# Spectra in DRAM regrouped by residue, natural blocks stored two at a time, and the filters' weights first in their pool

## The chip, the cores and the metric

The kernel runs on one core of a Trainium2 chip. The metric is device time in microseconds, from one launch, as the median of several runs; lower is better. A core has TensorE (PE in the profile; PEld are its weight loads), VectorE (DVE), ScalarE (ACT), GpSimd (POOL) and SyncE (SP). SP computes nothing: it issues DMA transfers. ScalarE issues some as well, in order with its own work. All transfers share 16 DMA engines.

## The reference

One layer of an encoder over 2048 positions and 1024 channels, float32: a projection feeds a long-convolution branch (Hyena, 512 channels) and an mLSTM branch; then come an output projection, cross-attention and a feed-forward block. The change touches the long convolution and one kind of output of the projection.

```python
def _hyena_filter_spectrum(L, w1, b1, fr1, w2, b2, fr2, w3):
    ...
    hid = jnp.sin(fr1 * (z @ w1 + b1))          # z: features of the position, (L, 33)
    hid = jnp.sin(fr2 * (hid @ w2 + b2))        # (L, 64)
    filt = (hid @ w3).reshape(L, HYENA_ORDER, FILTER_DIRS, D_HYENA)
    filt = filt * jnp.exp(-t * jnp.abs(deltas))[:, None, None, :]
    ...
    return jnp.fft.rfft(two_sided, axis=0)

def _hyena(hy, spec, skip):
    z, g1, g2 = u[..., :D_HYENA], u[..., D_HYENA:2 * D_HYENA], u[..., 2 * D_HYENA:]
    for o, gate in enumerate((g1, g2)):
        conv = jnp.fft.irfft(jnp.fft.rfft(z, n=2 * L, axis=1) * spec[:, o], n=2 * L, axis=1)[:, :L]
        z = gate * (conv + z * skip[o])
    return z
```

## The kernel before, in words

The transform of length 4096 is done by TensorE in two steps, with position n = 64 a + 16 q + j (a from 0 to 31, q from 0 to 3, j from 0 to 15). The first step (`front` for the filters, `spectrum` for the signal) transforms over a: for each j and q it gives 64 rows k (the frequency's low part, real and imaginary), 512 channels wide. The second step works by blocks, one for each k pair, with a 128 x 128 matrix over the 64 values of (q, j), real and imaginary. Between the steps the data must be regrouped from "by j" to "by k". That is done through DRAM: the tensors `fs0`, `fs1` hold the filters' spectra, `zs0`, `zs1` the signal's and `zg0`, `zg1` the product on its way back, 4 MB each, in the shape (64 k, 16 j, 4 q, 512).

- `by_phase` moves a piece between a tile of [128, 2, 512] (two values of j, 64 rows k each, two values of q) and DRAM. It issues two transfers of 64 partitions, 256 KB each, one for each j. It stores `fs` (in `front`, SP's queue) and `zs` (in `spectrum`, half on ScalarE's queue), and loads `zg` (in `load3`, SP).
- `of_block` names the block of one frequency: 64 rows (j, q) of 2 KB. A tile of [128, 2, 512] holds two blocks m = 0, 1, with the real part in partitions 0 to 63 and the imaginary part in 64 to 127. `load_filter` (`fs`) and `load2` (`zs`) fill such a tile with two transfers over 64 partitions, each with a half of both blocks; `back` stores `zg` with two, once both blocks are done.
- `natural` makes outputs of the projection in their natural layout, 128 positions by 256 columns at a time. Each is copied from PSUM to a tile `st` (three buffers, shared with `sweep_out`) and stored by ScalarE's queue with a transfer of 128 KB.
- `filters` makes the filters, and its tiles lie in the pool `f_sb`. `fw` are its weights and `hid` its hidden layer; both are last read by the products at L325. The tiles `a` (seven buffers) are the last to be stored. When `filters` ends the pool is closed, and the pool `h_sb` of `hyena` is opened at the same addresses: first `f1`, `e2` and `ghy`, then its ten buffers `a`, the first of which take the input tiles z. Tiles lie in a pool in the order in which they are first asked for.

The work of several generators is woven together by hand (`weave`, with weights), and a scheduler with a model of time then orders each engine's instructions and inserts semaphores. The main stream at that time is `sweep` and `natural`, the projection's products (L357, L360, L361), with the loads of `w_in` (`wn`, L397) and of the input (`xt`, L526) on SP's queue; `memproj` follows it (L726, its copies at L711). Each engine and each queue runs its own list in order.

Of the kernel before, what the change touches and what calls it, by code (L numbers as in the profile page):

```python
# [10 lines left out]
F32 = mybir.dt.float32  # L11
# [10 lines left out]
CH = 512  # L22
# [6 lines left out]
def shape_constants():  # L29
    f32 = np.float32  # L30
    ang = f32(TWO_PI / L) * np.arange(L, dtype=f32)
    tl = np.linspace(0.0, 1.0, L, dtype=f32)
    bands = np.linspace(1e-4, 15, 16, dtype=f32)
    arg = bands[:, None] * ang[None, :]
    feat = np.concatenate([tl[None], np.cos(arg), -np.sin(arg)], axis=0).astype(f32)
    back = (L - np.arange(L)) % L
    c_feat = np.concatenate([feat, feat[:, back]], axis=0)

    lo = math.log(1e-2) / 1.5
    hi = math.log(1e-2) / 0.3  # L40
    deltas = np.abs(np.linspace(lo, hi, CH, dtype=f32))
    win = np.exp(-(tl[:, None] * deltas[None, :]).astype(np.float64)).astype(f32)
    winb = win[back].copy()
    winb[0] = 0.0
    c_win = np.stack([win, winb], 0).reshape(2, 32, 4, 16, CH).transpose(0, 2, 1, 3, 4).reshape(2, L, CH)

    n1 = np.arange(32)
    kk = np.arange(16)
    f1 = np.zeros((2, 32, 4, 16, 2, 4))
    for par in range(2):  # L50
        th = 2 * np.pi * ((n1[:, None] * (2 * kk + par)[None, :]) % 64) / 64
        for h in range(4):
            f1[par, :, h, :, 0, h] = np.cos(th)
            f1[par, :, h, :, 1, h] = -np.sin(th)
            if par == 0:
                f1[0, :, h, 0, 1, h] = 1.0 - 2.0 * (n1 % 2)
    f1 = f1.reshape(2, 128, 128)
    wgt = np.full((2, 16, 2, 4), 2.0)
    wgt[0, 0] = 1.0
    e2 = f1.transpose(0, 2, 1) * (wgt.reshape(2, 128, 1) / 4096.0)  # L60
    own = f1.reshape(2, 32, 4, 16, 2, 4)[:, :, 0, :, :, 0].transpose(1, 0, 2, 3).reshape(32, 64)
    inv = e2.reshape(2, 16, 2, 4, 32, 4)[:, :, :, 0, :, 0].reshape(64, 32)

    n2 = np.arange(64).reshape(4, 16).T.reshape(64)
    k2 = np.arange(64)

    def block(freq):
        th = 2 * np.pi * ((n2[:, None] * freq[None, :]) % 4096) / 4096
        return np.cos(th), np.sin(th)

    dm = np.zeros((32, 2, 64, 2, 64))
    for par in range(2):
        for k in range(16):
            k1 = 2 * k + par
            b = dm[par * 16 + k]
            if k1 > 0:
                c, s = block(k1 + 64 * k2)
                b[0, :, 0], b[1, :, 0], b[0, :, 1], b[1, :, 1] = c, s, -s, c
            else:
                c, s = block(64 * k2[:32])  # L80
                b[0, :, 0, :32], b[0, :, 1, :32] = c, -s
                b[0, :, 1, 0] = 1.0 - 2.0 * (n2 % 2)
                c, s = block(32 + 64 * k2[:32])
                b[1, :, 0, 32:], b[1, :, 1, 32:] = c, -s
    dm = dm.reshape(32, 128, 128)
    em = dm.transpose(0, 2, 1).copy()
    two = np.full((128, 1), 2.0)
    two[0] = two[64] = 1.0
    em[0] *= two
    c = {  # L90
        "c_feat": c_feat,
        "c_win": c_win,
        "c_f1": np.tile(own, (4, 1)),
        "c_e2": np.tile(inv, (2, 1)),
        "c_dm": dm.transpose(1, 0, 2),
        "c_em": em.transpose(1, 0, 2),
    }
    return {k: np.ascontiguousarray(v.astype(np.float32)) for k, v in c.items()}
# [30 lines left out]
class Prog:  # L129
# [101 lines left out]

    def filters(self):
        nc, tc, a = self.nc, self.tc, self.a
        sd = [self.dram(f"fs{o}", (64, 16, 4, CH)) for o in range(2)]
        sb, ta, tb = self.fsb, self.ta, self.tb
        if True:
            fw = sb.tile([128, 1280], F32, name="fw")
            nc.sync.dma_start(out=fw, in_=a["fw"])
            w1, w2, w3 = fw[0:66, 0:128], fw[:, 128:256], fw[:, 256:1280].rearrange("p (o c) -> p o c", o=2)
            par = self.par[:, 128:132]  # L240
            for i in (0, 2):
                nc.vector.tensor_tensor(self.fb[:, i:i + 1], par[:, i:i + 1], par[:, i + 1:i + 2], ALU.mult)
            f1 = sb.tile([128, 128], F32, name="f1")[:, 0:64]
            nc.sync.dma_start(out=f1, in_=a["c_f1"])

            def sine(dst, src, b, fr, first=False):
# [10 lines left out]
                nc.vector.tensor_scalar(u, u, -PI_F, PI_F, ALU.max, ALU.min)  # L257
                nc.scalar.activation(dst, u if len(dst.shape) == 2 else u.rearrange("p (n q j) -> p n q j", q=4, j=16), AF.Sin)

            hid = sb.tile([128, 16, 128], F32, name="hid")  # L260
            def feat(c):
                t = tb()
                nc.sync.dma_start(out=t[0:66], in_=a["c_feat"][:, 512 * c:512 * c + 512])
# [53 lines left out]
            for j2 in range(8):  # L317
                yield 9
                (wf, wb), nxt = nxt, windows(j2 + 1)
                for o in range(2):  # L320
                    st, es = [ta() for h in range(2)], []
# [15 lines left out]
        self.fes.close()  # L337

    def by_phase(self, queue, d, j2, h, t, load=False):
        for jj in range(2):  # L340
            at, own = d[:, 2 * j2 + jj, 2 * h:2 * h + 2], t[64 * jj:64 * jj + 64]
            queue.dma_start(out=own if load else at, in_=at if load else own)

    def filters_open(self):
        self.fes = ExitStack()
        self.fsb = self.fes.enter_context(self.tc.tile_pool(name="f_sb", bufs=1))
        self.fsb.tile([128, 32], F32, name="f_even")

    def ta(self):
        return self.fsb.tile([128, 2, CH], F32, tag="a", name="a", bufs=7)  # L350
# [510 lines left out]
    def natural(self, hf, tiles, after=None, at=4):  # L861
        nc, a, sb = self.nc, self.a, self.isb
        xh, xl = self.xh, self.xl
        win = a["w_in"][0]
        for c2 in tiles:
            n = 256 if c2 < 3 else 272
            c0 = 2560 + 256 * c2
            wh, wl = next(self.wst)
            for t in range(8):
                if t % 4 == 0:  # L870
                    yield 11
                if c2 == tiles[-1] and after is not None:
                    if after is True and t == 0:
                        nxt = self.x_chunks(0)
                    if t == at:
                        if after is True:
                            self.prepq = nxt
                        else:
                            after()
                ts = slice(128 * t, 128 * t + 128)  # L880
                r0 = 1024 * hf + 128 * t
                p = self.mm()
                for k in range(8):
                    self.mm3(p[:, :n], xh[:, k, ts], xl[:, k, ts], wh[:, k, :n], wl[:, k, :n], k == 0, k == 7)
                if self.pending:
                    self.pending.pop(0)()
                self.pop()
                so = self.ist.tile([128, 512], F32, tag="st", name="st", bufs=3)[:, 0:256]
                if c2 < 2:
                    nc.scalar.copy(so, p[:, :256])  # L890
                else:
                    nc.scalar.activation(so, p[:, :256], AF.Sigmoid)  # L892
                nc.scalar.dma_start(out=(self.d_vd if c2 < 2 else self.d_od)[r0:r0 + 128, 256 * (c2 % 2):256 * (c2 % 2) + 256],
                                  in_=so)
                if c2 == 3:
                    sg = sb.tile([128, 16], F32, tag="sg", name="sg", bufs=2)
                    nc.vector.tensor_tensor(sg, p[:, 256:272], self.gb, ALU.add)
                    nc.sync.dma_start(out=self.d_gt[r0:r0 + 128], in_=sg)

    def hyena(self, es):  # L900
        nc, tc, a = self.nc, self.tc, self.a
        hy = self.dram("hy", (3, L, CH)).rearrange("s (n q j) c -> s q n j c", q=4, j=16)
        yh = self.dram("yh", (L, CH)).rearrange("(n q j) c -> q n j c", q=4, j=16)
        fs, sds, gds = ([self.dram(f"{n}{o}", (64, 16, 4, CH)) for o in range(2)] for n in ("fs", "zs", "zg"))
        own = [slice(64 * g, 64 * g + 64) for g in range(2)]
        phase = [slice(32 * q, 32 * q + 32) for q in range(4)]

        def of_block(d, g, k):
            return d[2 * k + g:2 * k + g + 3:2].rearrange("k j q c -> (j q) k c")

        sb = es.enter_context(tc.tile_pool(name="h_sb", bufs=1))

# [18 lines left out]
        def load_filter(o, i):  # L931
            dm = sb.tile([128, 2, 128], F32, tag="dm", name="dm", bufs=3)
            nc.sync.dma_start(out=dm, in_=a["c_dm"][:, 2 * i:2 * i + 2])
            t = ta()
            for g in range(2):
                nc.sync.dma_start(out=t[own[g]], in_=of_block(fs[o], g, 2 * i))
            return dm, t

        def load2(o, i):
            em = sb.tile([128, 2, 128], F32, tag="em", name="em", bufs=2)  # L940
            nc.sync.dma_start(out=em, in_=a["c_em"][:, 2 * i:2 * i + 2])
            t = ta()
            for g in range(2):
                nc.sync.dma_start(out=t[own[g]], in_=of_block(sds[o], g, 2 * i))
            return em, t

        def response(i, dm, t):
            hr, hi = ta(), ta()
# [31 lines left out]
        def back(m, i, em, y, gs, dst):  # L980
            pg = self.hy()
            nc.tensor.matmul(pg, em[:, m], y, start=True, stop=True)
            nc.scalar.copy(gs[:, m], pg)
            if m == 1:
                for g in range(2):
                    nc.scalar.dma_start(out=of_block(dst, g, 2 * i), in_=gs[own[g]])

        def spectrum(o, j2, z):
            st = [ta() for h in range(2)]
# [1198 lines left out]
```

## Time and profile before

| What | Value |
|---|---|
| median of 3 runs | 3108.53 us (3103.42 to 3110.13) |
| the profiled execution | 3105.18 us, span 3103.5 us |
| mean granted clock of TensorE | 0.984 |
| busy: PE, DVE, ACT, POOL | 2985.6, 1932.5, 1493.9, 1127.2 us |
| DMA | 607.08 MB in 446667 packets, mean 196 GB/s |
| transfers of 256 KB that touch `fs`, `zs`, `zg` | 64 each of stores and of loads, 384 in all |

The page is of one execution. A group's row gives line, engine, operation and tiles (output<-inputs), the count, the busy time and the mean of one in ns, then the idle time just before and what ended it. A row of waits reads "who <- whom: us in total, times, longest". In a table by stage each row is start:end, length, then busy time and count for each engine, the granted clock, the DMA engines' share in use and GB/s. "SPq" and "ACTq" are instructions that issue transfers; a transfer's row has the time that issuing took, not that of the data.

### The profile page before, as it was taken

How to read it: one execution, taken by the hardware profiler on the slowest of the kernel's cores; microseconds unless marked ns; L12 is line 12 of the kernel's file. 1: busy time of each engine (PE TensorE's matmuls, PEld its weight loads, DVE VectorE, ACT ScalarE, POOL GpSimd, SP SyncE). 2: the span in 40 equal slices, each digit the busy share in tenths (PEclk: the TensorE clock that was granted, in tenths of full speed). 3: DMA queues.
4: the chain of work that ended last, by engine and by line, in shares of the span. 5: the costliest groups of instructions: out<-in, count | busy, mean ns of one | idle time of the engine just before them, and what ended most of it. 6: DMA issues, size and time to landing. Idle time of an engine off the chain costs nothing.

```text
span 3103.5 us, 44160 instructions
## 1 busy us (share of the span) xinstructions
PE 2985.6 (96%) x14799; PEld 2367.6 (76%) x14799; DVE 1932.5 (62%) x3442; ACT 1493.9 (48%) x2930; POOL 1127.2 (36%) x798
## 2 busy tenths in 40 slices
PE   9999899998999798999999999999999999999998
PEld 7666566775577676888887888888888888888876
DVE  7865356556755445877664566557555676565695
ACT  6443356634753225565544455556555543333335
POOL 0121002200222323333132337766456375244653
PEclk9999999998999999999999999999999999999999
DMA  6555678687777996565476657657644565353434
GB/s 222 188 178 173 203 228 250 189 245 219 224 232 208 286 338 195 156 202 169 138 259 199 205 171 236 207 177 236 202 153 153 180 211 176 109 166 116 159 102 163
DMA packets 446667, 607.08 MB, mean 196 GB/s; under 512 B 41310, under 2 KB 251102, under 8 KB 445416
## 3 DMA queue, kind: packets, MB, share of 16 engines
q1 hardware_dynamic: 408292, 546.47, 56.1%
q10 hardware_dynamic: 38148, 57.79, 5.7%
q8 instruction: 117, 1.92, 0.3%
q14 instruction: 110, 0.90, 0.1%
HBM read 401.70 MB, written 202.41 MB: 195 GB/s over the span
## 4 chain that ended last, share of the span: by engine, by line
PE 56%; DVE 2%; DMA 1%; ACT 1%; issue 1%; POOL 0%; SPq 0%; DVEq 0%; ACTq 0%; POOLq 0%
PE mm L357 12%; PE mm L361 12%; PE mm L360 12%; PE hy L361 6%; PE hy L360 6%; PE hy L357 6%; PE hy L1319 1%; PE hy L1321 1%; DVE bl L1688 1%; PE hy L1591 0%; DVE acc L1986 0%; PE hy L1281 0%; PE hy L1197 0%; PE hy L1476 0%; DVE acc L2023 0%
## 5 line engine op out<-in xcount | busy, mean ns | idle before, releaser
L1687 ACT CAST ah<-w 128x512 fp32r<-128x512 f32 x284 | 176.7, 623 | 304.0 <-PE hy L360 155.8
L1688 DVE TENSOR_TENSOR bl<-wr,bh 128x512 fp32r<-128x512 f32 x213 | 235.0, 1108 | 128.1 <-ACT bh L1687 128.0
L368 DVE TENSOR_TENSOR wl<-wn,wh 128x512 fp32r<-128x512 f32 (+1 forms) x296 | 212.4, 762 | 98.7 <-ACT wh L368 98.5
L357 PE MATMUL mm<-xh,wh 128*128 128x512 f32 x640 | 267.6, 419 | 4.6 <-ACT xh L368 2.3
L1032 POOL TENSOR_TENSOR b<-b,a 128x512 f32<-128x512 f32 x64 | 85.7, 1341 | 494.7 <-ACT b L1030 466.6
L360 PE MATMUL mm<-xl,wh 128*128 128x512 f32 x640 | 256.5, 401 | 5.1 <-DVE xl L368 5.1
L361 PE MATMUL mm<-xh,wl 128*128 128x512 f32 x640 | 256.8, 402 | 0.0
L1687 ACT CAST bh<-wr 128x512 fp32r<-128x512 f32 x232 | 143.6, 621 | 226.1 <-PE mm L361 171.5
L1688 DVE TENSOR_TENSOR al<-w,ah 128x512 fp32r<-128x512 f32 x236 | 211.3, 896 | 53.5 <-ACT ah L1687 53.4
L361 PE MATMUL mm<-bh,al 128*128 128x512 f32 x576 | 223.6, 391 | 4.1 <-DVE al L1688 4.1
L357 PE MATMUL mm<-bh,ah 128*128 128x512 f32 x576 | 225.9, 392 | 0.1
L360 PE MATMUL mm<-bl,ah 128*128 128x512 f32 x576 | 225.1, 391 | 0.0
L368 ACT CAST wh<-wn 128x512 fp32r<-128x512 f32 (+1 forms) x296 | 164.4, 620 | 103.8 <-PE mm L361 49.9
L360 PE MATMUL mm<-act,wh 128*128 128x512 f32 x512 | 201.6, 394 | 0.0
L357 PE MATMUL mm<-act,wh 128*128 128x512 f32 x512 | 198.7, 394 | 2.2 <-ACT wh L368 2.1
L361 PE MATMUL mm<-act,wl 128*128 128x512 f32 x512 | 199.4, 391 | 0.0
L357 PE MATMUL hy<-bh,ah 128*128 128x512 f32 x448 | 175.2, 391 | 0.0
L360 PE MATMUL hy<-bl,ah 128*128 128x512 f32 x448 | 174.6, 390 | 0.0
L361 PE MATMUL hy<-bh,al 128*128 128x512 f32 x448 | 174.4, 390 | 0.0
L357 PEld LDWEIGHTS mm<-xh,wh 128*128 128x128 f32 x640 | 122.3, 191 | 57.0 <-issue 22.2
L357 PE MATMUL mm<-wh,xh 128*128 128x256 f32 (+1 forms) x512 | 156.7, 306 | 5.0 <-ACT st L892 2.2
L360 PEld LDWEIGHTS mm<-xl,wh 128*128 128x128 f32 x640 | 122.6, 192 | 47.1 <-issue 15.8
(380 smaller groups left out, 8080.3 us busy)
## 6 DMA issues: line engine op xcount, KB each, us to landing
wr<-hc SPq DMA_DIRECT2D x224, 256.0 KB
w<-in_ff_w_dram SPq DMA_DIRECT2D x172, 256.0 KB
hc<-wn SPq DMA_DIRECT2D x128, 256.0 KB
wn<-in_w_in_dram SPq DMA_DIRECT2D x100, 256.0 KB
hc<-q SPq DMA_DIRECT2D x96, 256.0 KB
fs<-a SPq DMA_DIRECT2D x64, 256.0 KB
a<-fs SPq DMA_DIRECT2D x64, 256.0 KB
a<-zs SPq DMA_DIRECT2D x64, 256.0 KB
```

Source lines behind the costliest of these rows:

```text
L357: first = mm(ps, lh, rh, start=start, stop=False)
L360: mm(ps, lh, rl, start=False, stop=False)
L361: self.last = mm(ps, ll, rh, start=False, stop=stop)
L368: both = (self.nc.scalar.copy(hi, src), self.nc.vector.tensor_tensor(lo, src, hi.bitcast(F32), ALU.subtract))
L1032: nc.gpsimd.tensor_tensor(xt, xt, hi[:, m], ALU.mult)
L1319: nc.tensor.matmul(dst, nm[:, h], va[:, h], start=True, stop=state is None)
L1321: nc.tensor.matmul(dst, rows_[d, 1][:, h], state[:, h], start=False, stop=True)
L1687: self.nc.scalar.copy(hi, src)
L1688: eng.tensor_tensor(lo, src, hi.bitcast(F32), ALU.subtract)
```

## The change

The DRAM tensors take the shape (16 j, 64 k, 4 q, 512), and the 128 rows of a block go from the order (g, j, q), with g the real or imaginary half, to (j, g, q), so the matrices `dm` and `em` have their rows permuted on the host. A piece of `by_phase` becomes one transfer of 128 partitions and 512 KB. A block of one m becomes one transfer of 128 partitions and 256 KB (16 stretches of 16 KB, 512 KB apart in DRAM), loaded by the new `load_block` and stored by `back` as soon as that block is done. `natural` keeps two blocks in one tile `st` and stores them together, 256 KB. `fw`, `hid` and `f1` are asked for when the pool `f_sb` is opened, ahead of its tiles `a`.

```diff
@@ shape_constants
-    n2 = np.arange(64).reshape(4, 16).T.reshape(64)
+    n2 = np.arange(64)
...
-    dm = dm.reshape(32, 128, 128)
+    dm = dm.reshape(32, 2, 4, 16, 128).transpose(0, 3, 1, 2, 4).reshape(32, 128, 128)
@@ filters
-        sd = [self.dram(f"fs{o}", (64, 16, 4, CH)) for o in range(2)]
+        sd = [self.dram(f"fs{o}", (16, 64, 4, CH)) for o in range(2)]
...
-            fw = sb.tile([128, 1280], F32, name="fw")
+            fw, hid, f1 = self.f_w, self.f_hid, self.f_f1
...
     def by_phase(self, queue, d, j2, h, t, load=False):
-        for jj in range(2):
-            at, own = d[:, 2 * j2 + jj, 2 * h:2 * h + 2], t[64 * jj:64 * jj + 64]
-            queue.dma_start(out=own if load else at, in_=at if load else own)
+        at = d[2 * j2:2 * j2 + 2, :, 2 * h:2 * h + 2].rearrange("j k q c -> (j k) q c")
+        queue.dma_start(out=t if load else at, in_=at if load else t)
...
     def filters_open(self):
...
         self.fsb.tile([128, 32], F32, name="f_even")
+        self.f_w = self.fsb.tile([128, 1280], F32, name="fw")
+        self.f_hid = self.fsb.tile([128, 16, 128], F32, name="hid")
+        self.f_f1 = self.fsb.tile([128, 128], F32, name="f1")[:, 0:64]
@@ natural
-                so = self.ist.tile([128, 512], F32, tag="st", name="st", bufs=3)[:, 0:256]
+                if t % 2 == 0:
+                    st = self.ist.tile([128, 2, 256], F32, tag="st", name="st", bufs=3)
+                so = st[:, t % 2]
...
-                nc.scalar.dma_start(out=(self.d_vd if c2 < 2 else self.d_od)[r0:r0 + 128, 256 * (c2 % 2):256 * (c2 % 2) + 256],
-                                  in_=so)
+                if t % 2:
+                    dst = (self.d_vd if c2 < 2 else self.d_od)[r0 - 128:r0 + 128, 256 * (c2 % 2):256 * (c2 % 2) + 256]
+                    nc.scalar.dma_start(out=dst.rearrange("(t p) c -> p t c", p=128), in_=st)
@@ hyena
-        fs, sds, gds = ([self.dram(f"{n}{o}", (64, 16, 4, CH)) for o in range(2)] for n in ("fs", "zs", "zg"))
+        fs, sds, gds = ([self.dram(f"{n}{o}", (16, 64, 4, CH)) for o in range(2)] for n in ("fs", "zs", "zg"))
...
-        def of_block(d, g, k):
-            return d[2 * k + g:2 * k + g + 3:2].rearrange("k j q c -> (j q) k c")
+        def of_block(d, i, m):
+            k = 4 * i + 2 * m
+            return d[:, k:k + 2].rearrange("j g q c -> j (g q) c")
+
+        def load_block(d, i):
+            t = ta()
+            for m in range(2):
+                nc.sync.dma_start(out=t[:, m], in_=of_block(d, i, m))
+            return t
...
         def load_filter(o, i):
...
-            t = ta()
-            for g in range(2):
-                nc.sync.dma_start(out=t[own[g]], in_=of_block(fs[o], g, 2 * i))
-            return dm, t
+            return dm, load_block(fs[o], i)
...
         def back(m, i, em, y, gs, dst):
...
             nc.scalar.copy(gs[:, m], pg)
-            if m == 1:
-                for g in range(2):
-                    nc.scalar.dma_start(out=of_block(dst, g, 2 * i), in_=gs[own[g]])
+            nc.scalar.dma_start(out=of_block(dst, i, m), in_=gs[:, m])
```

`load2` is changed as `load_filter` is, with `zs`.

The counts of PE, VectorE and GpSimd instructions stay; their order changes from the filters to the end of `hyena` and is the same behind it. Three places. The first is SP's queue at the end of the filters: `fs1<-a` are the last filter stores, `wn` the projection's weights, `f1`, `e2` and `a<-hy` the first loads of the new stage. Before:

```order
L838 DMA qt_76<-cv_3301 128x1008
L342 DMA fs1_389<-a_2652 64x1024 x2
L342 DMA fs1_389<-a_2653 64x1024 x2
L921 DMA f1_2776<-in_c_f1_dram 128x64
L922 DMA e2_2777<-in_c_e2_dram 128x32
L928 DMA a_2782<-hy_75 32x1024 x4
```

And now:

```order
L838 DMA qt_76<-cv_3269 128x1008
L339 DMA fs1_392<-a_2624 128x1024
L339 DMA fs1_392<-a_2625 128x1024
L397 DMA wn_3548<-in_w_in_dram 128x2x256
L397 DMA wn_3552<-in_w_in_dram 128x2x256
L397 DMA wn_3556<-in_w_in_dram 128x2x256
L397 DMA wn_3560<-in_w_in_dram 128x2x256
L931 DMA f1_2744<-in_c_f1_dram 128x64
L932 DMA e2_2745<-in_c_e2_dram 128x32
L938 DMA a_2750<-hy_75 32x1024 x4
```

Four weight loads have moved ahead of the stage's first loads. In both, `f1` is the instruction that waits for the last two pieces of `fs1` to land; the rows behind it need no wait of their own for that. On PE, at the same place, the last filter product (`hy<-b,f`, with 15 more) and the first spectrum product (`hy<-a,f`, with 7 more) have the projection's products between them, of which the end is shown here. Before:

```order
L357 MATMUL mm<-xh,wh 128x512
L360 MATMUL mm<-xl,wh 128x512
L361 MATMUL mm<-xh,wl 128x512
L173 MATMUL hy<-a,f_2776 64x512
L186 MATMUL hy<-a,f_2776 64x512 x7
```

And now:

```order
L173 MATMUL hy<-b,f_110 32x512
L186 MATMUL hy<-b,f_110 32x512 x15
L361 MATMUL mm<-xh,wl 128x512
L357 MATMUL mm<-xh,wh 128x512
L360 MATMUL mm<-xl,wh 128x512
L361 MATMUL mm<-xh,wl 128x512
L173 MATMUL hy<-a,f_2744 64x512
L186 MATMUL hy<-a,f_2744 64x512 x7
```

Where 12 products of the projection stood between the two, 4 are left; the other 8 come later. The second place is VectorE at the sixth spectrum, whose results it copies (`a<-hy`), between the projection's weights (`wl`) and its convolution (`cv`). Before:

```order
L368 TENSOR_TENSOR wl_3587<-wn_3600,wh_3586 128x512
L799 SCALAR_TENSOR_TENSOR cv_3581<-P_3465,par_70,cv_3581 128x1008
L995 COPY a_3610<-hy_3613 128x512
L995 COPY a_3610<-hy_3614 128x512
L800 SCALAR_TENSOR_TENSOR cv_3581<-P_3465,par_70,cv_3581 128x1008
```

And now:

```order
L368 TENSOR_TENSOR wl_3547<-wn_3560,wh_3546 128x512
L997 COPY a_3570<-hy_3573 128x512
L997 COPY a_3570<-hy_3574 128x512
L799 SCALAR_TENSOR_TENSOR cv_3541<-P_3429,par_70,cv_3541 128x1008
L800 SCALAR_TENSOR_TENSOR cv_3541<-P_3429,par_70,cv_3541 128x1008
```

The two copies have moved ahead of the convolution's first step. The third place is SP's queue at the first `load3` pieces (`a<-zg0`, with the gate `a<-hy`), beside two loads of the input (`xt`). Before:

```order
L342 DMA a_5637<-zg0_2771 64x1024 x2
L342 DMA a_5638<-zg0_2771 64x1024 x2
L969 DMA a_5643<-hy_75 32x1024 x4
L342 DMA a_5931<-zg0_2771 64x1024
L526 DMA xt_5810<-in_x_t_dram 128x2x512
L342 DMA a_5931<-zg0_2771 64x1024
L526 DMA xt_5844<-in_x_t_dram 128x2x512
L342 DMA a_5932<-zg0_2771 64x1024 x2
L969 DMA a_5937<-hy_75 32x1024 x4
```

And now:

```order
L339 DMA a_5565<-zg0_2739 128x1024
L339 DMA a_5566<-zg0_2739 128x1024
L973 DMA a_5569<-hy_75 32x1024 x4
L339 DMA a_5849<-zg0_2739 128x1024
L339 DMA a_5850<-zg0_2739 128x1024
L973 DMA a_5853<-hy_75 32x1024 x4
L339 DMA a_5870<-zg0_2739 128x1024
L339 DMA a_5871<-zg0_2739 128x1024
L526 DMA xt_5732<-in_x_t_dram 128x2x512
```

The input's loads have moved from the middle of the second piece to behind the third piece's loads.

More of the change, by code (lines that the diff above doesn't have):

```diff
@@ L242, in filters @@
                 nc.vector.tensor_tensor(self.fb[:, i:i + 1], par[:, i:i + 1], par[:, i + 1:i + 2], ALU.mult)
-            f1 = sb.tile([128, 128], F32, name="f1")[:, 0:64]
             nc.sync.dma_start(out=f1, in_=a["c_f1"])
@@ L258, in sine @@
                 nc.scalar.activation(dst, u if len(dst.shape) == 2 else u.rearrange("p (n q j) -> p n q j", q=4, j=16), AF.Sin)
-            hid = sb.tile([128, 16, 128], F32, name="hid")
             def feat(c):
@@ L941, in load2 @@
             nc.sync.dma_start(out=em, in_=a["c_em"][:, 2 * i:2 * i + 2])
-            t = ta()
-            for g in range(2):
-                nc.sync.dma_start(out=t[own[g]], in_=of_block(sds[o], g, 2 * i))
-            return em, t
+            return em, load_block(sds[o], i)
         def response(i, dm, t):
@@ L983, in back @@
             nc.scalar.copy(gs[:, m], pg)
-            if m == 1:
-                for g in range(2):
-                    nc.scalar.dma_start(out=of_block(dst, g, 2 * i), in_=gs[own[g]])
+            nc.scalar.dma_start(out=of_block(dst, i, m), in_=gs[:, m])
         def spectrum(o, j2, z):
```

## The prediction

> **What bounds the kernel now.** I read the page, then the busy time by stage, then TensorE's (PE's) waits stage by stage, then the queues around the longest waits. The span says how much can be won at all:
>
> ```profile
> span 3103.5 us, 44160 instructions
> PE 2985.6 (96%) x14799; PEld 2367.6 (76%) x14799; DVE 1932.5 (62%) x3442; ACT 1493.9 (48%) x2930; POOL 1127.2 (36%) x798
> ```
>
> PE is idle for 117.9 us. The change removes no PE instruction (14799 stay), so it can win only idle time and the slow clock beside it. The stages (start:end, busy time of each engine, granted clock, share of the DMA engines in use, GB/s):
>
> ```profile
> 159.00:350.00 191.00, 191.00 (x1200) 131.94 (x1200) 107.53 (x161) 78.91 (x137) 37.23 (x26) 0.99 0.58 171
> 350.00:450.00 100.00, 82.87 (x413) 55.98 (x413) 44.05 (x69) 45.70 (x74) 5.15 (x3) 0.90 0.83 251
> 450.00:634.00 184.00, 178.30 (x970) 132.43 (x969) 102.52 (x159) 111.86 (x203) 38.25 (x30) 0.99 0.71 210
> 634.00:760.00 126.00, 108.58 (x720) 76.84 (x718) 75.24 (x157) 46.79 (x79) 0.00 (x0) 0.91 0.89 254
> 760.00:970.00 210.00, 203.02 (x953) 144.44 (x952) 129.90 (x265) 127.54 (x222) 48.96 (x38) 1.00 0.69 202
> 970.00:1110.00 140.00, 118.63 (x689) 96.28 (x687) 67.90 (x185) 39.23 (x77) 50.16 (x38) 0.94 0.98 294
> 1160.00:3103.50 1943.50, 1906.55 (x8886) 1581.98 (x8884) 1252.48 (x2103) 934.58 (x1934) 919.71 (x641) 0.99 0.55 178
> ```
>
> I call them F (filters), A (first spectra), B (first convolution), C (its end and the second spectra), D (second convolution), E (its end) and the rest. PE's idle time is 0 in F, 17.1 us in A, 5.7 in B, 17.4 in C, 7.0 in D and 21.4 in E. C and E are also where the DMA engines are nearly full and the clock sags. What ended PE's waits between 340 and 1110 us (total, times, longest):
>
> ```profile
> PE mm L726 <- ACT kt L711: 12.8, 4, 5.0
> PE hy L173 <- DMA a<-hy: 11.5, 1, 11.5
> PE hy L173 <- issue: 8.3, 3, 5.3
> PE hy L173 <- DMA a<-zg: 6.6, 3, 4.2
> PE hy L1027 <- DMA a<-zs: 6.4, 2, 5.5
> PE mm L951 <- DMA a<-fs: 5.9, 2, 3.8
> ```
>
> The zg waits and the longest zs and fs waits lie in C, the kt waits in E. The first spectrum's wait of 11.5 us is in A.
>
> **The change part by part.** *What a transfer costs.* SP's and ScalarE's queues, spectra transfers first (issue time in ns, minimum/median/maximum), and one load that covers 128 partitions:
>
> ```profile
> L342 SPq DMA_DIRECT2D fs<-a x64: 451/588/1922, 122.2 to 354.4; - x64
> L342 SPq DMA_DIRECT2D a<-zg x64: 445/586/1726, 634.2 to 1094.3; - x64
> L944 SPq DMA_DIRECT2D a<-zs x64: 573/617/2053, 423.7 to 928.8; - x64
> L986 ACTq DMA_DIRECT2D zg<-a x64: 582/616/1421, 451.7 to 968.9; - x64
> L294 SPq DMA_DIRECT2D a<-in_c_win_dram x16: 347/438/1807, 69.9 to 283.7; - x16
> ```
>
> A transfer over 64 partitions takes at least 445 to 582 ns to issue, one over 128 at least 347. `by_phase` becomes one 512 KB transfer for two of 256 KB: about 2 x 0.59 down to 0.44, 0.7 us of queue for each of 96 pieces. Nearly all of that is hidden in F, where PE never waits; it counts in C and E, where SP is in front of PE. The block transfers stay two of 256 KB, but each now holds one whole frequency, so PE's first product needs one landed transfer where it needed both. Their own issue time is between 0.35 (full width) and 0.62 us (as now); I take 0.5, because they still carry three-dimensional patterns.
>
> *What a byte costs.* GB/s by DMA share, in two stretches ruled by half-width transfers and two by full-width ones:
>
> ```profile
> 640.00:690.00 50.00, 45.09 (x346) 35.42 (x345) 27.26 (x50) 14.99 (x28) 0.00 (x0) 0.93 0.99 271
> 975.00:1000.00 25.00, 25.00 (x148) 19.41 (x147) 15.38 (x37) 6.13 (x9) 8.50 (x5) 1.00 1.01 262
> 1110.00:1145.00 35.00, 35.00 (x184) 27.65 (x183) 17.40 (x48) 8.15 (x16) 10.50 (x8) 1.00 1.03 340
> 1850.00:2950.00 1100.00, 1098.35 (x4845) 908.05 (x4844) 678.70 (x847) 504.24 (x844) 634.36 (x435) 1.00 0.55 178
> ```
>
> At a full share the first two move 274 and 259 GB/s (mean 267), the last two 330 and 324 (mean 327). So a spectrum byte gets at most 1.22 times cheaper (327/267), and perhaps not at all, since the input and gate loads over 32 partitions in the same stretches stay. [...]
>
> *Stage A, the first input tile.* The filters' weights now stand first in their pool, so the second stage's first tiles lie over weights instead of over tiles that are stored last. SP, ScalarE, VectorE and PE there (start, us, what):
>
> ```profile
> 352.64 2.77 SPq L342 DMA_DIRECT2D fs<-a  x4
> 358.20 0.37 SPq L921 DMA_DIRECT2D f<-in_c_f_dram  x1
> 359.08 5.65 SPq L928 DMA_DIRECT2D a<-hy  x12
> ...
> 351.57 2.02 ACT L313 COPY a<-hy 128x512 f32<-128x512 f32 x4
> ...
> 354.14 2.50 DVE L368 TENSOR_TENSOR wl<-wn,wh 128x512 fp32r<-128x512 f32 x4 [3.44 <-ACT wh L368]
> ...
> 349.81 0.50 PE L357 MATMUL mm<-xh,wh 128*128 128x512 f32 x1
> ...
> 352.43 0.39 PE L361 MATMUL mm<-xh,wl 128*128 128x512 f32 x1
> 364.32 1.08 PE L173 MATMUL hy<-a,f 32*64 32x512 f32 x1 [11.50 <-DMA a<-hy]
> ```
>
> SP ends the last four filter stores at 355.41 and can issue nothing of the new stage until 358.20, when they have landed (2.8 us). In the changed kernel the load of `f1` still waits for the last two filter stores, so the new place does not set it free. The last store is issued at about 354.0 (the copies end at 353.59) and lands at about 356.8. But four weight loads now stand between the stores and `f1`; each needs a buffer that VectorE's L368 frees, the last at 356.64, so `f1` goes out at about 357.0: 1.2 us earlier. Against it, PE has 4 matmuls where it had 12 (349.81 to 352.82, 0.25 us each) to cover the wait: 8 x 0.25 = 2.0 us more to do afterwards. Sum +0.8 us; the ends are -1.2 (the cover is not missed) and +5.2 (the 1 MB of weights also delays the tile by 1 MB at 327 GB/s, 3.2 us). I stay near the low end, since those 3.2 us run from 354.8 on, mostly before the tile's packets. The other wait in A is ended by copies:
>
> ```profile
> 397.39 1.27 DVE L799 SCALAR_TENSOR_TENSOR cv<-P,par,cv 128x1008 f32<-128x1008 f32 x1 [0.80 <-ACT cv L797]
> 398.57 1.28 DVE L995 COPY a<-hy 128x512 f32<-128x512 f32 x2
> 399.95 1.08 PE L173 MATMUL hy<-a,f 32*64 32x512 f32 x1 [5.29 <-issue]
> ```
>
> The copies now stand ahead of L799, so 1.2 us go; then ScalarE's half of the copies ends the wait. A comes to -0.4.
>
> *Stage C.* Three effects. First, the longest zg wait (4.2 us) is for the second piece's loads, and SP is seen there putting 2 x 512 KB of `x_t` between them:
>
> ```profile
> 639.01 0.45 SPq L342 DMA_DIRECT2D a<-zg  x1
> 640.12 0.40 SPq L526 DMA_DIRECT2D xt<-in_x_t_dram  x1
> 643.49 0.40 SPq L526 DMA_DIRECT2D xt<-in_x_t_dram  x1
> 645.09 3.55 SPq L969 DMA_DIRECT2D a<-hy  x4
> ```
>
> They now stand behind the third piece's loads. 1 MB at 271 GB/s is 3.9 us, so that wait goes (-3.7). The clock is worth some more: if it falls to one half when it falls, 0.91 over 126 us is half clock for 23 us, of which at most 17.4 can be idle, so at least 5.6 us of work run at half speed, 2.8 us lost over five or so waits; at most 11 are. I take 2 for this one. Second, the other zg waits (2.4 us) lose an issue each (-1.0). Third, the waits for fs (3.8) and zs (5.5) hang on a store, then a load: one store issue less (-0.6 for zs), and half the data before the first product (256 KB at 271 GB/s, 0.9 us) with one issue less (0.5): -1.4 for fs and -2.0 for zs. Sum -10. Bounds: 0, if the copies ahead of the stores set these waits, and -28, all idle time (17.4) with the clock's upper value.
>
> *Stage E.* The DMA share of 0.98 says that the stage is as long as its bytes. Its zg loads are 8.4 MB (that pass's 32 transfers of 256 KB): 31.4 us at 267 GB/s, 25.7 at 327, so -5.7 at most and 0 at least. I take -4, since the kt waits (12.8) are ScalarE waiting on stores and loads in that queue, -2 for the clock (0.94), and -1 for the paired natural stores, whose buffers are asked for half as often. Sum -7, ends 0 and -13.
>
> *B and D.* B has no DMA wait on PE; fewer stalls of ScalarE's queue (32 natural stores and 16 of 32 zs stores gone, all beside PE's work) give -1. D's waits for fs (2.1) and zs (0.8) lose 2. F: 0, hidden behind a PE that is never idle there, with 42% of the DMA share free; if that cover goes, the order rival below is what comes. The host's matrices and the addresses cost nothing: same shapes, same counts. Total: -0.4 -1 -10 -2 -7 = -20.4.
>
> The profiled execution took 3105.2 us (span 3103.5 and 1.7 around it) against a median of 3108.5 in the runs. 3105.2 - 20.4 = 3084.8 on the profile's scale, 3088 on the median's.
>
> **The rivals.** *Nothing moves (3106).* The waits in C and E are set by PSUM copies and by small loads over 32 partitions, which stay. For it: the first wait in A keeps its barrier, and the kt waits are ended by ScalarE, not by a spectra transfer. Against: 15.9 of C's 17.4 us of idle time end with a DMA on a spectrum. Worth -2.
>
> [...]
>
> *The new layout is slower to read (3155).* A block is now 16 pieces of 16 KB that lie 512 KB apart, where it was 128 KB in a row. B and D last 394 us at a share of 0.70: 118 us of DMA are free, and 50 MB of spectra pass there (192 transfers of 256 KB), 187 us at 267 GB/s. It decides from 50/(187 + 118), 164 GB/s, downwards; at half speed (133) it costs 187 - 118 = 69 us, less the 20 elsewhere. Against: no row shows such a distance. [...]
>
> *The new order opens waits (3117).* The scheduler reorders PE, VectorE and ScalarE from 150 to 1110 us. In F alone PE had no gap; six new waits of 3 us and 2 for the clock (30 us) outweigh the sum.
>
> **How the numbers follow.** Forecast 0.50 (own range 3074 to 3100), all waits go 0.15, nothing moves 0.19, new order 0.09, slow layout 0.07. A difference under 0.2% (6.2 us) can't be told from none here. Faster by more: 0.50 + 0.15 + 0.03 of the third = 0.68; same 0.17; slower 0.15. The time is that of the likeliest, 3088. The range runs from 3062, the all-waits case, to 3112, past the case where nothing moves.
>
> **What would show it.** Right: the zg wait of 4.2 us in C is gone, fs and zs waits shorter by 1 to 2 us each, GB/s at a full share above 290 in the first zg loads, issue of L339 near 0.4 us, the first spectrum's wait still 11 to 14 us, the kt waits near 9. Wrong: gaps of PE between 160 and 350 us, a first wait under 6 us (the barrier was not what held it), or a block load that takes longer than now.

## The result, and the profile after

| | before | after |
|---|---|---|
| median | 3104.14 us (10 runs, 3099.12 to 3110.13) | 3095.36 us (10 runs, 3088.15 to 3100.51) |
| the profiled execution | 3105.18 us | 3100.22 us |
| granted clock | 0.984 | 0.984 |

The ratio is 0.9966, with a 95% interval from 0.9955 to 0.9977: the change takes off 7 to 14 us of 3104, about 10.6 (the two medians alone differ by 8.8). The forecast was 20.4 less. The sign held, and so did the relief of the DMA engines; the size was about half.

The page of the changed kernel, its span and busy time:

```profile
span 3098.5 us, 44022 instructions
PE 2989.6 (96%) x14799; PEld 2371.5 (77%) x14799; DVE 1945.6 (63%) x3442; ACT 1494.4 (48%) x2930; POOL 1121.0 (36%) x798
```

PE's idle time is 108.9 us, where it was 117.9: 9.0 less. This pair of executions differs by 5.0 us in span, since PE's busy time, with the same instructions, came out 4.0 longer; the runs differ from one to the next by as much, so effects of this size are read from the ratios, and one pair of profiles tells only roughly where they sit. The stages, F, A, B, C, D, E and the rest (start:end, length, busy time by engine, granted clock, DMA share, GB/s):

```profile
159.00:350.00 191.00, 190.91 (x1208) 131.00 (x1208) 107.76 (x162) 80.17 (x139) 35.66 (x26) 1.00 0.52 171
350.00:450.00 100.00, 84.61 (x418) 56.87 (x418) 48.39 (x76) 49.15 (x80) 5.61 (x4) 0.90 0.78 262
450.00:634.00 184.00, 180.00 (x1014) 135.81 (x1012) 103.11 (x157) 112.09 (x201) 37.17 (x28) 0.99 0.70 215
634.00:760.00 126.00, 111.15 (x707) 78.30 (x697) 76.56 (x167) 47.03 (x81) 3.84 (x2) 0.93 0.78 245
760.00:970.00 210.00, 200.53 (x938) 142.28 (x937) 128.03 (x253) 126.29 (x219) 47.80 (x37) 0.99 0.68 205
970.00:1110.00 140.00, 124.61 (x733) 102.00 (x732) 73.48 (x203) 37.70 (x76) 49.48 (x40) 0.95 0.98 310
1160.00:3098.50 1938.50, 1901.60 (x8844) 1578.24 (x8842) 1257.96 (x2086) 930.21 (x1916) 912.89 (x637) 0.99 0.55 177
```

Two things can be worked out from them, beside the same rows of before:

| | F | A | B | C | D | E |
|---|---|---|---|---|---|---|
| PE idle, before (us) | 0 | 17.1 | 5.7 | 17.4 | 7.0 | 21.4 |
| PE idle, after | 0.1 | 15.4 | 4.0 | 14.9 | 9.5 | 15.4 |
| forecast of the difference, clock left out | 0 | -0.4 | -1 | -8 | -2 | -5 |
| GB/s over DMA share, before | 295 | 302 | 296 | 285 | 293 | 300 |
| GB/s over DMA share, after | 329 | 336 | 307 | 314 | 301 | 316 |

GB/s over DMA share is what the engines would move with all of them busy. By it a byte got 1.10 to 1.12 times cheaper in F, A and C, and 1.03 to 1.05 times in E and in B and D, where of the spectra's transfers only blocks pass. The DMA engines were relieved as forecast; PE got little of it. Over the six stages PE's idle time falls by 9.4 us, from 68.6 to 59.2. How it is shared among them is less certain: e2 below, which gains nothing, has 21.8 us of idle time in C and 16.7 in E, 4.4 more and 4.6 less than the kernel before. PE's waits, the costliest that touch the change:

```profile
PE hy L173 <- DMA a<-hy: 11.7, 1, 11.7
PE mm L726 <- ACT kt L711: 7.6, 2, 3.9
PE hy L1029 <- DMA a<-zs: 7.5, 3, 4.0
PE hy L173 <- ACT a L997: 5.4, 2, 3.7
PE hy L173 <- DVE a L1050: 5.3, 2, 4.6
PE hy L173 <- DMA a<-zg: 0.6, 1, 0.6
```

The waits for zg (6.6 us) are all but gone, and no row is left for fs (5.9). Two rows are new: PE now waits for copies of a spectrum (ScalarE's L997) and for the gate's product (VectorE's L1050, formerly L1048). The queues:

```profile
L339 SPq DMA_DIRECT2D fs<-a x32: 319/341/955, 123.0 to 352.0; - x32
L339 SPq DMA_DIRECT2D a<-zg x32: 319/400/1585, 626.0 to 1080.6; - x32
L918 SPq DMA_DIRECT2D a<-zs x64: 514/597/1408, 419.2 to 924.2; - x64
L988 ACTq DMA_DIRECT2D zg<-a x64: 524/526/613, 438.6 to 963.4; - x64
```

A piece's one transfer takes 319 ns or more to issue, 341 and 400 at the median, where 0.44 us was assumed. A block's transfer, also 128 partitions wide, takes 514 ns or more and gains little on the 573 of a half-width one; its DRAM side is 16 stretches, and e5 below has the price of a single one.

### The profile page after: what moved, and what is told of

Its sections match the earlier page's. It is cut to its first block, busy times and chain, and to the rows that moved or that the text cites. A ratio compares the mean times of both kernels' runs of the same rounds, so it can differ in the third digit from the quotient of the medians.

```text
span 3098.5 us, 44022 instructions
## 1 busy us (share of the span) xinstructions
PE 2989.6 (96%) x14799; PEld 2371.5 (77%) x14799; DVE 1945.6 (63%) x3442; ACT 1494.4 (48%) x2930; POOL 1121.0 (36%) x798
## 4 chain that ended last, share of the span: by engine, by line
PE 81%; DMA 9%; DVE 6%; issue 2%; ACT 1%; SPq 1%; POOL 0%; ACTq 0%; DVEq 0%; POOLq 0%
PE mm L357 17%; PE mm L361 17%; PE mm L360 17%; PE hy L357 6%; PE hy L361 6%; PE hy L360 6%; PE hy L173 2%; PE hy L1029 2%; PE hy L986 2%; PE mm L955 2%; DMA a<-zg 1%; PE mm L709 1%; PE hy L1321 1%; DMA xt<-in_x_t_dram 1%; PE hy L1323 1%
```

## The experiments

Ratios are to the kernel before, with 95% intervals.

| | edit | median (us) | ratio | interval |
|---|---|---|---|---|
| e1 | changed, spectra's layout only | 3094.33 | 0.9965 | 0.9951 to 0.9979 |
| e2 | before, natural stores in pairs | 3104.76 | 0.9999 | 0.9989 to 1.0009 |
| e3 | before, weights placed first | 3105.13 | 0.9993 | 0.9983 to 1.0003 |
| e4 | changed, pieces of half width | 3098.04 | 0.9975 | 0.9965 to 0.9985 |
| e5 | before, blocks of full width | 3097.07 | 0.9977 | 0.9967 to 0.9987 |
| e6 | e5, loads only | 3099.10 | 0.9982 | 0.9974 to 0.9991 |
| e7 | e5, one load for two blocks | 3091.88 | 0.9962 | 0.9949 to 0.9975 |
| e8 | changed, first tiles in a pool of their own | 3076.84 | 0.9912 | 0.9897 to 0.9927 |
| e9 | e7 with wide pieces in the old order | 3777.74 | 1.2173 | 1.2156 to 1.2189 |
| e10 | e9 with the pool of e8 | 3772.58 | 1.2154 | 1.2137 to 1.2170 |
| e11 | changed, natural stores issued by SP | 3090.36 | 0.9956 | 0.9944 to 0.9968 |
| e12 | e8 and e11 together | 3079.45 | 0.9913 | 0.9899 to 0.9927 |

**Which edit carries it (e1, e2, e3).** Each of the three edits alone; e2 and e3 put one edit of the diff into the kernel before, and e1 takes both of these out of the changed one.

> Of the three edits only the layout of the spectra (one transfer over 128 partitions for each piece); the natural blocks are stored one by one and the filters' weights stand where they stood before. The kernel before took 3104 us and the changed one 3095 (-0.34%). Theory 1 (the wide pieces carry the gain): 3094 to 3097, ratio 0.997, idle time of PE from 970 to 1110 us near 15 us. Theory 2 (the three edits share the gain): 3099 to 3101, ratio near 0.9985. Theory 3 (the paired natural stores cost something, since ScalarE stood 8.7 us at one of them from 663 us on): faster than the changed kernel, 3088 to 3092, and the 4.6 us gap of PE at 680 us is gone.

> The kernel before with the paired natural stores alone. Theory 1: no change, 3102 to 3106. Theory 2: -2 to -4 us by half as many stores on ScalarE's queue. Theory 3 (a paired store holds ScalarE longer): +2 to +6 us.

> The kernel before with the weights placed first alone. The prediction gave it +0.8 -1.2 us: 3103 to 3105, and the wait of PE for the first input tile stays at 11 to 13 us. The rival, that the first input tile comes free: the wait falls under 6 us, and the time to 3096 to 3099.

The layout of the spectra gives the whole gain (e1 0.9965, the full change 0.9966); pairs and place give nothing that can be measured. Theory 3 falls: e1 stores the natural blocks one by one and still has the gap of PE near 680 us (5.1 us).

**Which transfer carries it (e4 to e7).** e4 moves a piece in two halves again:

```diff
-        at = d[2 * j2:2 * j2 + 2, :, 2 * h:2 * h + 2].rearrange("j k q c -> (j k) q c")
-        queue.dma_start(out=t if load else at, in_=at if load else t)
+        for jj in range(2):
+            at, own = d[2 * j2 + jj, :, 2 * h:2 * h + 2], t[64 * jj:64 * jj + 64]
+            queue.dma_start(out=own if load else at, in_=at if load else own)
```

> The changed kernel with each piece of a spectrum again moved as two transfers of 64 partitions (the new layout in DRAM, the block transfers and the two other edits stay). If the width of the pieces carries the gain: back to 3101 to 3105, issue of L339 near 0.58 us, zg waits of PE over 4 us from 634 to 760 us. If the order in DRAM or the block transfers carry it: 3094 to 3097.

Neither: 3098.0, between the two. Some three quarters of the gain stay without wide pieces (0.25% of 0.34%), and the intervals of the two kernels overlap. So e5 widens the block transfers alone, in the order of before, where two rows of k are one stretch of 256 KB. As in the changed kernel, each load then holds one whole block, and each block of zg is stored as soon as it is done:

```diff
-        def of_block(d, g, k):
-            return d[2 * k + g:2 * k + g + 3:2].rearrange("k j q c -> (j q) k c")
+        def of_block(d, i, m):
+            k = 4 * i + 2 * m
+            return d[k:k + 2].rearrange("g j q c -> (g j q) c")
...
```

> The kernel before with wide block transfers alone: two transfers of 128 partitions (one for each pair of rows, 256 KB in a row in DRAM) in place of two of 64, for the loads of fs and zs and the stores of zg; pieces, their order in DRAM, natural blocks and the filters' place as before. With half-width pieces the changed kernel kept 0.25% of its 0.34%. If the block transfers carry that: 3097 to 3100, ratio 0.9975. If the order in DRAM carries it (a piece's rows 8 KB apart instead of 128 KB): 3104 to 3107, ratio 0.999 to 1.000.

> As the run with wide block transfers, but only the loads of fs and zs are wide; the stores of zg stay two of 64 partitions after the second half. If the loads carry the gain: within 2 us of that run. If the stores of zg do (ScalarE issues them, and the first row of a pair leaves one product earlier): 3104 to 3107.

e7 loads both blocks of a tile at once:

```diff
+            nc.sync.dma_start(out=t, in_=d[4 * i:4 * i + 4].rearrange("(m g) j q c -> (g j q) m c", g=2))
...
```

> As the run with wide block transfers, but a block of fs or zs is one load of 512 KB. If width carries the gain: the same time as that run, or 1 to 2 us less (one issue of 0.5 us less for each block). If the first product's earlier start does (its half of the block lands first): 2 to 6 us more, and longer waits of PE for fs and zs.

(e6 leaves the stores of zg as two of 64 partitions.) e5 is at 0.9977 with no piece touched: by the ratios the block transfers carry about two thirds, and their loads most of that (e6), though the intervals overlap. That the first product could start on half of the block isn't the reason: e7 loads the whole block at once and is no slower. At 0.9962 e7 gains as much as the whole change, with the old order in DRAM, the old pieces and neither of the other two edits. How much of it is width and how much is issue was not separated. B and D in e5 (this execution, of 3106.87 us, was the longest of e5's twelve, so shares and issue times are read from it, not its length):

```profile
450.00:634.00 184.00, 178.76 (x973) 132.99 (x972) 102.22 (x161) 113.67 (x205) 39.68 (x30) 0.99 0.65 214
760.00:970.00 210.00, 200.64 (x936) 141.52 (x935) 124.17 (x251) 124.94 (x216) 46.28 (x36) 0.98 0.62 201
```

and its block transfers:

```profile
L915 SPq DMA_DIRECT2D a<-zs x64: 319/430/1645, 424.7 to 929.5; - x64
L985 ACTq DMA_DIRECT2D zg<-a x64: 321/326/375, 448.2 to 967.8; - x64
```

By GB/s over share that is 329 and 324, where the changed kernel has 307 and 301, and an issue takes 319 ns where it takes 514. A block in one stretch is thus the cheaper one by a few per cent; the new order buys the cheap piece with a dearer block.

**The first input tile (e8).** The first two input tiles, `f1` and `e2` lie in a pool of their own, over space that the earlier pool `x_o` has left by then, and are loaded from `filters`, at j2 = 6.

```diff
+    def hyena_open(self):
+        self.hes = ExitStack()
+        self.hp = self.hes.enter_context(self.tc.tile_pool(name="h_first", bufs=1, side="right"))
...
+    def hyena_first(self):
...
+        for j2 in range(2):
+            for q in range(4):
+                nc.sync.dma_start(out=self.h_z[j2][32 * q:32 * q + 32], in_=hy[0, q, :, 2 * j2:2 * j2 + 2])
...
-        q, fq = [load1(0), load1(1)], []
+        q, fq = [self.h_z[0], self.h_z[1]], []
```

> The changed kernel with f1, e2 and the first two input tiles of the second stage in a pool of their own, over space that is free since about 160 us, and loaded before the last filter stores. If the wait at 363 us (11.7 us) comes from the pool that those tiles lie in: the first spectrum starts near 353 us, the wait is under 1 us, and the time is 3084 to 3089 (-7 to -11). If the wait only moves to the third tile: 3093 to 3096.

Faster than either end: 17 us below the changed kernel by the two ratios (18.5 by the medians, which come from different series). SP's queue and PE's first spectrum in the changed kernel:

```profile
351.07 1.30 SPq L339 DMA_DIRECT2D fs<-a  x2
353.29 2.17 SPq L397 DMA_DIRECT2D wn<-in_w_in_dram  x4
355.64 0.34 SPq L931 DMA_DIRECT2D f<-in_c_f_dram  x1
356.72 7.84 SPq L938 DMA_DIRECT2D a<-hy  x12
...
362.67 1.08 PE L173 MATMUL hy<-a,f 32*64 32x512 f32 x1 [11.69 <-DMA a<-hy]
```

and in e8 the loads of the two tiles (issue time, first and last start), PE's first spectrum, and stages A and E:

```profile
L922 SPq DMA_DIRECT2D z<-hy x8: 323/420/706, 213.7 to 217.1; - x8
```

```profile
351.24 0.64 PE L173 MATMUL hy<-z,f 32*64 32x512 f32 x1 [1.10 <-ACT a L311]
```

```profile
350.00:450.00 100.00, 94.06 (x461) 63.96 (x461) 56.24 (x91) 56.46 (x92) 8.19 (x6) 0.97 0.82 275
970.00:1110.00 140.00, 130.09 (x761) 106.43 (x760) 68.75 (x191) 37.36 (x77) 50.70 (x41) 0.96 0.99 320
```

The loads go out 140 us earlier, and the wait falls from 11.7 to 1.1 us. PE gains 9.5 us of busy time in A, and 5.5 in E, where it was not aimed. The branch starts 11 us earlier, is 13 us ahead at its first zg load (613.0 against 626.0 us) and 29 at its last (1051.3 against 1080.6); that its last loads now meet other work is a likely reason for E, which was not tested. So here a first tile that is really free was worth more than the whole diff. The weights-first place doesn't give it. With the place alone (e3), `f1` still waits for the four last filter stores on SP's queue, and PE's first wait is 11.55 us:

```profile
SPq L922 <- DMA fs<-a: 2.7, 4, 1.0
```

In the changed kernel `f1` goes out 2.6 us earlier (355.64 against 358.20 us), behind 1 MB of weights, and the first spectrum starts 1.7 us earlier (362.67 against 364.32).

**Both orders' best at once (e9, e10).** Old order in DRAM, so that blocks are one stretch and take one load as in e7, and pieces in one transfer all the same, its slowest dimension now the two values of j; e10 adds the pool of e8.

```diff
-        at = d[2 * j2:2 * j2 + 2, :, 2 * h:2 * h + 2].rearrange("j k q c -> (j k) q c")
+        at = d[:, 2 * j2:2 * j2 + 2, 2 * h:2 * h + 2].rearrange("k j q c -> j k (q c)")
...
```

> The changed kernel with the old order of the spectra in DRAM: pieces are still one transfer over 128 partitions (its rows now 128 KB apart), and a block of fs or zs is one load of 512 KB (before: two of 64 partitions; changed: two of 256 KB). The old order with one load a block and half-width pieces gave 3092 (0.9962). If wide pieces are worth their 3 us whatever the order in DRAM: 3088 to 3091. If the order with a piece's rows side by side is what made wide pieces worth anything: 3092 to 3095.

> The same with the first two input tiles, f1 and e2 in a pool of their own (that alone brought the changed kernel from 3095 to 3077). If the two gains add up: 3070 to 3074. If the free tile's gain in the last stages is the same time that one load a block saves: 3075 to 3079.

Both theories of e9, and both of e10, missed by a fifth of the whole time; e10 is only 5 us below e9. The stages F and B of e9, and then its longest waits of PE:

```profile
159.00:350.00 191.00, 125.69 (x710) 83.15 (x711) 67.18 (x98) 46.00 (x80) 24.56 (x16) 0.81 0.31 104
450.00:634.00 184.00, 76.14 (x409) 50.33 (x407) 35.94 (x54) 33.73 (x53) 4.73 (x3) 0.68 0.31 102
```

```profile
PE hy L173 <- DMA a<-zg: 147.4, 9, 22.2
PE hy L173 <- DMA a<-hy: 87.4, 4, 39.5
```

F, where PE had never waited, has 65 us of idle time, at a DMA share of only 0.31 and 104 GB/s: most of the DMA engines stand idle while everything waits for them. e9 differs from e7 in this form of the pieces and in the two edits that e2 and e3 found to be worth nothing, so the form is the cause. In two stretches pieces are the last transfers issued and nothing else is seen under way, two of `fs` issued from 239.4 us on and two of zg from 939.9 on:

```profile
243.00:252.00 9.00, 2.69 (x12) 1.88 (x10) 0.00 (x0) 0.00 (x0) 0.00 (x0) 0.93 0.13 51
945.00:952.00 7.00, 0.00 (x0) 0.00 (x0) 0.00 (x0) 0.00 (x0) 0.00 (x0) 0.50 0.13 53
```

A share of 0.13 is as much as 2 busy engines of 16 would give (0.125). No row here tells which engines carried a transfer, and why this form leaves most of them idle was not shown.

**ScalarE behind its own store (e11, e12).** In stage C of the changed kernel, ScalarE, VectorE and PE:

```profile
672.41 0.37 ACTq L897 DMA_DIRECT2D od<-st  x1
672.88 0.66 ACT L894 ACTIVATE st<-mm 128x256 f32<-128x256 f32 x2 [8.72 <-DMA a<-zg]
673.30 0.17 DVE L900 TENSOR_TENSOR sg<-mm,par 128x16 f32<-128x16 f32 x1 [8.93 <-ACT st L894]
677.21 0.17 DVE L900 TENSOR_TENSOR sg<-mm,par 128x16 f32<-128x16 f32 x1 [3.74 <-DMA gt<-sg]
677.42 0.69 DVE L1050 TENSOR_TENSOR a<-hy,a 128x512 f32<-128x512 f32 x1
679.96 1.11 PE L173 MATMUL hy<-a,f 32*64 32x512 f32 x1 [4.62 <-DVE a L1050]
```

ScalarE stops 8.7 us at the issue of a natural store, until zg loads have landed; VectorE's `sg` waits for ScalarE and then for its own small stores; the gate's product L1050 stands behind `sg`, and PE waits for it. e11 issues these stores from SP:

```diff
-                    nc.scalar.dma_start(out=dst.rearrange("(t p) c -> p t c", p=128), in_=st)
+                    nc.sync.dma_start(out=dst.rearrange("(t p) c -> p t c", p=128), in_=st)
```

> The changed kernel with the paired natural stores issued by SP instead of ScalarE. ScalarE stood 8.7 us at such a store from 663 us on, and PE waited 4.6 us behind it. If that wait costs the kernel: the PE gap near 680 us is gone and the time is 3088 to 3093. If the wait only moves (ScalarE then stops at its next transfer, or SP holds back loads while it waits for ScalarE's copies): 3094 to 3100.

```profile
677.50 0.64 PE L173 MATMUL hy<-a,f 32*64 32x512 f32 x1 [3.50 <-DVE a L1050]
```

The gap shrinks to 3.5 us and does not go. The median is 5 us lower, but the interval (0.9944 to 0.9968) overlaps that of the changed kernel, so the gain itself isn't settled.

> The changed kernel with the two edits that helped: the first two input tiles, f1 and e2 in a pool of their own (3077 alone), and the paired natural stores issued by SP (3090 alone, 5 us under the changed kernel). If they take away different waits: 3070 to 3074, and no wait of PE over 4 us from 600 to 760 us. If the second only shortened the first's waits: 3075 to 3079.

Together they give what e8 gives alone, and a wait of 4.8 us of PE for the gate's product is left in this stretch (at 665.6 us). e8 and e12 are the best versions that were run, 0.9912 and 0.9913.

## Why the prediction was half right

The measured 3095.36 us lies inside the stated range, 3062 to 3112, which holds the kernel before (3104.14) as well. The forecast of 3088 stood on a median of three runs, 3108.53; that of ten is 4.4 us lower. The sum of the six stages, with the clock left out, was -16.4 us of idle time, and -9.4 came: C and D fell short by 9.9, and A, B and E together gave 3.0 more than forecast.

- *Stage A, the first tile* (+0.8 forecast): right that the barrier stays. The wait is 11.7 us (11.5 before), and e3 shows no gain. `f1` goes out 2.6 us earlier, not 1.2. The other wait in A, for copies behind L799, fell from 5.3 to 3.7 us (-1.2 forecast).
- *What a byte costs* (at most 1.22 times cheaper): right; 1.03 to 1.12. The sign "over 290 GB/s at a full share in the first zg loads" is not clear: 282 from 636 to 660 us at a share of 1.00, but 295 at 0.96 from 626 to 676 us. No run shows bytes so cheap that all of the DMA's waits go, the case that sets the low end of the range (3062, a chance of 0.15): they became 1.03 to 1.12 times cheaper, and 59.2 of the 68.6 us of PE's idle time in the six stages stayed. No run here times a transfer alone.
- *Which transfers gain.* The sum gave 9.3 us to the pieces (3.7, 1.0 and 0.6 in C, 4 in E) and 4.8 to the blocks (1.4 and 1.4 in C, 2 in D). The runs point the other way: 0.25% of the 0.34% stay without wide pieces (e4), and wide blocks alone give 0.23% (e5). With overlapping intervals this is a reading of the ratios, not a proof.
- *Issue of a block's transfer* (0.5 us taken, a value near the wide end of 0.35): mis-sized. It is 0.60 for the loads of zs (median) and 0.53 for stores. Width isn't what prices it: e5's are as wide and take 0.43 and 0.33.
- *Stage C* (-10, of it 2 for the clock): this term failed. The waits that it named did shrink, zg from 6.6 to 0.6, fs from 3.8 to none, zs from 5.5 to 2.2, and even by more than forecast; but C's idle time fell by 2.6 only, from 17.42 to 14.85, since L1050, the copies of L997 and a wait of 3.9 us put down to issue came in their place:

```profile
PE hy L173 <- DVE a L1050: 5.3, 2, 4.6
PE hy L173 <- issue: 3.9, 1, 3.9
PE hy L1029 <- DMA a<-zs: 2.2, 1, 2.2
PE hy L173 <- ACT a L997: 1.7, 1, 1.7
PE hy L173 <- DMA a<-zg: 0.6, 1, 0.6
```

The other runs agree: e1 has no zg or fs wait in C either, with zs back at 5.5, and 17.7 us of idle time; e4 to e7 have 13.5 to 15.3. The bound of 0 had been given for a case near this one, "if the copies ahead of the stores set these waits". The sum took off each wait in full without asking what ends next. The clock went from 0.91 to 0.93.

- *Stage D* (-2): it came to +2.5. A zs wait of 4.0 us and one of 2.4 for VectorE's L1035 stand where 2.9 us of fs and zs waits stood. The dearer block of the new order passes there, but the runs do not bear it out as the cause: e1, with the same blocks, has 6.3 us of idle time in D, and e5, with blocks in one stretch, 9.4. Why D differs stays open.
- *Stage E* (-7, of it 2 for the clock): right in size. Idle time fell by 6.0, the kt waits from 12.8 to 7.6 us. That cheaper bytes did it is not shown, since E is at 16.7 in e2, without them.
- *Paired stores* (-1, in E): nothing that the time shows (e2).
- *The rivals.* The slow layout did not come: the block transfers are no slower to issue than before (the loads of zs 0.60 us at the median against 0.62), B and D move as much (215 and 205 GB/s against 210 and 202). Nor did the new order cost anything in F, where PE is busy for 190.91 of 191 us. By their own terms and 3108.5 the times of these two come to 3157 and 3118, not 3155 and 3117; nothing hangs on it.

## What to carry to other kernels

Take a forecast wait off only down to the next thing that is late: add up what each engine still needs before that instruction, and count only the difference. Before a tile is moved to a better address, look at what its first load waits for; if it is the closing of a pool, a small pool of its own for the first tiles can be worth more than a better address (here 17 us against nothing that could be measured). When a transfer is widened, try the form of its DRAM side first: with two half-width pieces (64 rows each, 128 KB apart) joined in one transfer this kernel took a fifth longer (e9, 1.217). Before data is laid out anew, try the cheaper form of the transfers in the old layout: e7 gained as much as the whole change.

## What the runs showed of the hardware

- With two half-width pieces (64 rows each, 128 KB apart in DRAM) joined in one transfer of 128 partitions and 512 KB the kernel took 1.217 times as long, at a DMA share of 0.31 in stage F and 0.13 (51 to 53 GB/s) where nothing else is seen under way (e9). In the changed kernel, whose pieces are 128 rows 8 KB apart, PE is busy for 190.91 of the 191 us of stage F (share 0.52, 171 GB/s).
- Transfers over 128 partitions took differently long to issue: 319 ns at least where the DRAM side is one stretch of 256 KB (the loads of zs in e5) or 128 evenly spaced rows (pieces of the changed kernel), 514 where it is 16 stretches of 8 rows (its loads of zs). The half-width loads of zs in the kernel before took at least 573.
- In the changed kernel ScalarE stopped for 8.7 us at the issue of a store, and the profile puts the end of that wait down to zg loads of SP's queue. What ties the two together the profile doesn't say.
